# Unsplit float32 operands for 128-column attention products, and a later place for retention's row scaling

## The chip, the core and the metric

The kernel runs on one core of one Trainium2 chip. The metric is the time of one execution on the device in microseconds (us); the kernel before takes 961.94 us, the median of 3 runs (961.93 to 963.8). TensorE (PE in the profile, PEld for its weight loads) multiplies matrices, VectorE (DVE), ScalarE (ACT) and GpSimd (POOL) work on elements, SyncE (SP) issues DMAs; each engine works through its own queue in order.

## The reference

Two layers of a decoder trunk, on 512 tokens of width 1024, all in float32. In each layer one input projection of the normed residual feeds four groups, each 512 wide: retention (4 heads of 128), a Mamba-2 state-space mixer (8 heads of 64), stick-breaking attention (4 heads of 128) and cross-attention to 256 memory tokens (4 heads of 128). Each group is gated, and one output projection maps the concatenation back. The two groups that the change touches:

```
retention, per head, with q, k after rope:
    y[n] = sum over m <= n of  decay(n - m) * (q[n] . k[m]) * v[m]
    y    = (y - mean(y)) / sqrt(var(y) + 1e-6)          # per token, over the head's 128 columns

stick-breaking, per head, with z = q k^T / sqrt(128):
    w[n, m] = exp( z[n, m] - sum over j = m..n-1 of softplus(z[n, j]) )   for m < n, else 0
    y[n]    = sum over m of w[n, m] * v[m]
```

## The kernel before

**Split products.** A float32 matrix `a` is kept as two tiles in the reduced format that TensorE reads (fp32r): `h`, a rounded copy that ScalarE writes, and `l = a - h`, which VectorE writes (`split`, lines 285 to 287). A product is then three matmuls into one bank, h·h, h·l and l·h (`mm3`, lines 280 to 283, all through `mm`, line 278). The input and output projections, which are most of the work, are done so too: `pj<-hTh,wh`, `pj<-hTl,wh` and `pj<-hTh,wl` in the profile, with 512 columns or, for some, 256.

**Causal blocks.** 512 tokens are 4 blocks of 128, so causal products shrink in steps of 128 columns. Stick-breaking computes for query block t the scores against keys 0 to 128(t+1), that is 128, 256, 384 and 512 columns (`sb_head`, lines 629 to 653): three matmuls, then one bf16 matmul that adds the mask to the diagonal block, then Abs, Exp and Ln on ScalarE, a max, a scan and a subtract on VectorE, and a last Exp. `sb_head2` transposes the weights on TensorE (line 661) and splits them, `sb_head3` multiplies them by the values (512 down to 128 columns). Retention (`ret_head`, lines 718 to 733) computes scores of 512 down to 128 columns, splits each, and GpSimd zeroes the upper triangle of the diagonal block in both halves (line 730); `ret_head2` multiplies by the values, and squares and sums. So each head of either kind has one score product and one value product with 128 columns.

**Retention's norm.** `ret_head3` sums the squares over the head's columns with one matmul against a column of ones (`mx<-r,onesr`); its operand is written by VectorE at line 747. The resulting row of 512 goes through `row_rstd` (lines 702 to 716): ScalarE copies it, a DMA folds it to 32 partitions (`t<-r`), GpSimd adds eps and takes the power -0.5 (`t`, lines 710 and 711), a DMA writes it to DRAM (`row<-t`) and a last one broadcasts it to 128 partitions (`r<-row`). Then VectorE multiplies the head's output with it (`scaled`, line 757).

**What sets the order.** The code runs over projections in a fixed order; each projection is one unit, and `defer(n, f)` puts a function off until n units later, so that the attention work lies between projections. That is only a priority: a scheduler in the compiler then chooses, with a model of the engines, the order in which each engine's queue holds the instructions, except where the code asks for program order. Banks of PSUM come from two pools of four, `pj` for projections and `mx` for the rest. Tiles in SBUF come from pools of equal slots: 33 of class `s`, 16 of `y`, 9 of `r`.

Of the kernel before, what the change touches and what calls it, by code (L numbers as in the profile page):

```python
# [11 lines left out]
AF = mybir.ActivationFunctionType  # L12
# [4 lines left out]
P = 128  # L17
SEQ = 512
NT = SEQ // P
# [4 lines left out]
HEADS = 4  # L24
HD = 128
GW = 512
EPS = 1e-6
SCALE = HD ** -0.5
# [100 lines left out]
RP, RJ = 32, 16  # L129
# [34 lines left out]
def v3(ap, a):  # L164
    return ap.rearrange("p (a b) -> p a b", a=a)


class Builder:
# [384 lines left out]
    def scaled_pair(self, b, scale):  # L553
# [58 lines left out]
    def sb_v(self, l):  # L612
        nc = self.nc
        banks = self.proj_a(extra=SSD_H, turns=l == 0)
        if l:
            self.behind(self.turn[3], self.marks[1])
        first = [Pair(self), Pair(self)]
        u = self.tiny(32)
        uv = u.rearrange("p (h c) -> p c h", c=4)
        bias = self.par(l, "dtb", 0, 32).rearrange("p (h c) -> p c h", c=4)  # L620
        for t, b in enumerate(banks):
            p, c = first[t // 2], slice(256 * (t % 2), 256 * (t % 2) + 256)
            self.split(b[:, :256], p.h[:, c], p.l[:, c], p.hf[:, c])
            nc.vector.tensor_add(uv[:, t], b[:, 256:256 + SSD_H], bias[:, t])
        self.defer(1, self.dt_chain, l, u)
        second = [self.pair(b) for b in self.proj_a()]
        return [[first[i], second[i]] for i in range(2)]

    def sb_head(self, h, v):
        nc = self.nc  # L630
        q = self.scaled_pair(self.proj_b(), SCALE)
        k = self.pair(self.proj_b())
        w = [t[:, c] for t, c in self.packed([P * (t + 1) for t in range(NT)], self.buf)]
        for t in range(NT):
            n = P * (t + 1)
            ts = slice(P * t, P * t + P)
            b = self.mx()[:, :n]
            self.mm(b, q.h[:, ts], k.h[:, :n], True, False)
            self.mm(b, q.h[:, ts], k.l[:, :n], False, False)
            self.mm(b, q.l[:, ts], k.h[:, :n], False, False)  # L640
# [12 lines left out]
        return y  # L653

    def sb_head2(self, h, v, w, y):
        nc = self.nc
        wT = self.pairs_packed([SEQ - P * j for j in range(NT)])
# [5 lines left out]
        self.defer(1, self.sb_head3, h, v, wT, y)  # L663

    def sb_head3(self, h, v, wT, y):
        b = self.mx()
        for j in range(NT):
            c = slice(P * j, SEQ)
            self.mm3(b[:, c], *self.vcols(v, j, h), wT[j][0], wT[j][1], j == 0, j == NT - 1)
        self.nc.scalar.copy(y, b)  # L670


    def ret_v(self):

        nc = self.nc
        ginv = self.con("ginv", 16)
        out = [[None, None], [None, None]]
        for half in range(2):
            for i, b in enumerate(self.proj_a()):
                st = self.tiny(4)  # L680
                nc.vector.tensor_reduce(out=st, in_=v3(b, 4), op=ALU.add, axis=AX.X)
                nc.vector.tensor_scalar(out=st, in0=st, scalar1=-1.0 / HD, scalar2=None, op0=ALU.mult)
                vt = self.buf()
                for j in range(4):
                    t, h = 2 * i + j // 2, 2 * half + j % 2
                    nc.vector.tensor_scalar(out=vt[:, P * j:P * j + P], in0=b[:, P * j:P * j + P],
                                            scalar1=st[:, j:j + 1], scalar2=ginv[:, 4 * t + h:4 * t + h + 1],
                                            op0=ALU.add, op1=ALU.mult)
                out[i][half] = self.pair(vt)
        return out  # L690

    def rope(self, b):
        nc = self.nc
        cos, sin = self.con("cos", SEQ), self.con("sin", SEQ)
        A, B = self.buf(), self.buf()
        nc.vector.tensor_tensor(out=B[0:64], in0=b[64:128], in1=sin[64:128], op=ALU.mult)
        nc.vector.tensor_tensor(out=B[64:128], in0=b[0:64], in1=sin[0:64], op=ALU.mult)
        nc.vector.tensor_tensor(out=A, in0=b, in1=cos, op=ALU.mult)
        nc.vector.tensor_add(A, A, B)
        return self.pair(A)  # L700

    def row_rstd(self, row, eps):

# [14 lines left out]
    def ret_head(self, h, v):  # L718
        nc = self.nc
        q = self.rope(self.proj_b())  # L720
        k = self.rope(self.proj_b())
        sc = self.pairs_packed([SEQ - P * c for c in range(NT)])
        for c in range(NT):
            n = SEQ - P * c
            cs, ms = slice(P * c, SEQ), slice(P * c, P * c + P)
            b = self.mx()[:, :n]
            self.mm3(b, k.h[:, ms], k.l[:, ms], q.h[:, cs], q.l[:, cs], True, True)
            self.split(b, *sc[c])
            for d in (sc[c][0][:, :P], sc[c][1][:, :P]):
                nc.gpsimd.affine_select(out=d, in_=d, pattern=[[1, P]], compare_op=ALU.is_ge, fill=0.0, base=0, channel_multiplier=-1)  # L730
        y = self.buf(tag="y")
        self.defer(4, self.ret_head2, h, v, sc, y)
        return y

    def ret_head2(self, h, v, sc, y):
        nc = self.nc
        b = self.mx()
        for c in range(NT):
            self.mm3(b[:, P * c:], *self.vcols(v, c, h), sc[c][0], sc[c][1], c == 0, c == NT - 1)
        nc.scalar.copy(y, b)  # L740
        sq = [self.buf(tag="r")[0:64] for _ in range(2)]
        for i in range(2):
            nc.scalar.activation(sq[i], b[64 * i:64 * i + 64], AF.Square, scale=HD ** -0.5)
        nc.vector.tensor_add(sq[0], sq[0], sq[1])
        z = self.new(512, F32R, "r")
        nc.scalar.copy(z[0:64], sq[0])
        nc.vector.tensor_sub(z[64:128], sq[0], z[0:64].bitcast(F32))
        self.defer(1, self.ret_head3, h, z, y)

    def ret_head3(self, h, z, y):  # L750
        nc = self.nc
        vb = self.mx()[0:1]
        self.mm(vb, self.onesr[:, 0:1], z[:], True, True)
        self.defer(5, self.scaled, y, self.row_rstd(vb, self.con("reps", HEADS * RJ, RP)[:, RJ * h:RJ * h + RJ]))

    def scaled(self, y, rB):
        self.nc.vector.tensor_mul(y, y, rB)


    def dt_chain(self, l, u):  # L760
# [437 lines left out]
```

## Time and profile before

| | |
|---|---|
| median of 3 runs | 961.94 us (961.93 to 963.8) |
| the profiled execution | 961.89 us |
| its span, first to last instruction | 960.2 us |
| lies outside the span | 1.69 us |
| TensorE's mean granted clock | 0.998 |
| stick-breaking, about | 123 to 205 us, and again some 471 us later in layer 2 |
| retention, with the state-space group between, about | 205 to 330 us, and again 471 us later |

A timeline gives start, length, engine, line, operation, tiles written and read, shape, and how many like instructions stand in a row; in brackets the engine's idle time before it and what ended it. TensorE's matmuls are pipelined, and their lengths overlap: how fast it works is read from start to start, not from the lengths. A product of unsplit float32 operands is shown as two matmul records.

### The profile page before, as it was taken

What the parts mean: (1) busy time and instruction counts of PE and PEld (TensorE: products, weight loads), DVE (VectorE), ACT (ScalarE), POOL (GpSimd) and SP (SyncE); (2) the same over time, 40 slices, a digit from 0 to 9 for tenths busy, and PEclk for the clock granted to TensorE, in tenths of its full rate; (3) what the DMA queues carried; (4) which work ended last, traced back from release to release, by engine and by line L of the source; (5) the groups of instructions that cost most, each with busy time, mean ns of one, the idle gap of its engine ahead of it and who ended that gap; (6) DMA issues with size and microseconds to landing.
All of it is one profiled execution on the core that took longest, in us unless ns stands there. A gap on an engine that the chain in (4) does not pass through costs nothing.

```text
span 960.2 us, 13253 instructions
## 1 busy us (share of the span) xinstructions
PE 949.8 (99%) x5151; PEld 812.6 (85%) x5151; DVE 657.4 (68%) x1056; ACT 456.8 (48%) x844; POOL 104.4 (11%) x160
## 2 busy tenths in 40 slices
PE   9999999999999999999999999999999999999997
PEld 7998889988887888888899888898888878888885
DVE  5855567767777796854487465768777968877443
ACT  6544566534554342643465345665344543435341
POOL 1100000001231201100040000000003421102001
PEclk9999999999999999999999999999999999999999
DMA  9442212122232524344344222112222333423502
GB/s 347 149 147 80 88 45 88 45 88 88 91 108 99 165 88 121 115 160 142 120 170 184 89 88 71 62 45 88 77 78 85 134 105 116 120 91 120 195 25 87
DMA packets 26734, 105.79 MB, mean 110 GB/s; under 512 B 4144, under 2 KB 4400, under 8 KB 17456
## 3 DMA queue, kind: packets, MB, share of 16 engines
q10 hardware_dynamic: 10224, 73.44, 21.8%
q1 hardware_dynamic: 16448, 31.52, 10.0%
q8 instruction: 40, 0.66, 0.3%
q14 instruction: 22, 0.18, 0.1%
HBM read 100.63 MB, written 4.28 MB: 109 GB/s over the span
## 4 chain that ended last, share of the span: by engine, by line
PE 88%; DVE 5%; DMA 3%; ACT 1%; issue 1%; POOL 1%; DVEq 0%; SPq 0%; ACTq 0%; POOLq 0%
PE pj L278 65%; PE mx L278 22%; DVE s L647 1%; DMA r<-row 1%; PE mx L599 1%; PE mx L449 1%; DMA mem<-memT 1%; DMA s<-acs 1%; DVE wl L287 1%; DMA t<-r 1%; POOL t L711 1%; DVE s L810 1%; DVE s L646 0%; PE mx L661 0%; DVE s L287 0%
## 5 line engine op out<-in xcount | busy, mean ns | idle before, releaser
L278 PE MATMUL pj<-hTh,wh 128*128 128x512 f32 x704 | 277.5, 394 | 0.0
L278 PE MATMUL pj<-hTl,wh 128*128 128x512 f32 x704 | 276.6, 393 | 0.0
L278 PE MATMUL pj<-hTh,wl 128*128 128x512 f32 x704 | 275.4, 391 | 0.0
L287 DVE TENSOR_TENSOR wl<-raw,wh 128x1024 fp32r<-128x1024 f32 (+2 forms) x155 | 183.7, 1190 | 114.2 <-ACT wh L286 107.3
L286 ACT CAST wh<-raw 128x1024 fp32r<-128x1024 f32 (+2 forms) x155 | 158.0, 1025 | 178.9 <-PE pj L278 153.7
L278 PEld LDWEIGHTS pj<-hTh,wl 128*128 128x128 f32 x704 | 132.3, 188 | 26.7
L278 PEld LDWEIGHTS pj<-hTh,wh 128*128 128x128 f32 x704 | 132.3, 188 | 26.4
L278 PEld LDWEIGHTS pj<-hTl,wh 128*128 128x128 f32 x704 | 132.4, 188 | 25.7
L278 PE MATMUL pj<-wh,s 128*128 128x512 f32 (+1 forms) x384 | 99.8, 355 | 0.0
L278 PE MATMUL mx<-s,s 128*128 128x256 f32 (+4 forms) x616 | 97.5, 310 | 0.3
L278 PEld LDWEIGHTS mx<-s,s 128*128 128x128 f32 (+1 forms) x616 | 84.6, 178 | 12.9 <-issue 3.1
L278 PE MATMUL mx<-wh,s 128*128 128x512 f32 x256 | 79.2, 389 | 0.0
L278 PEld LDWEIGHTS pj<-wh,s 128*128 128x128 f32 x384 | 66.1, 189 | 10.5
L730 POOL TENSOR_SCALAR_AFFINE_SELECT s<-s 128x128 fp32r<-128x128 f32 x64 | 21.2, 363 | 420.6 <-DVE s L287 420.6
L278 PE MATMUL pj<-wl,s 128*128 128x512 f32 (+1 forms) x192 | 63.4, 354 | 0.0
L278 PE MATMUL pj<-wh,hTh 128*128 128x256 f32 (+1 forms) x208 | 60.3, 290 | 0.5 <-DVE s L556 0.5
L287 DVE TENSOR_TENSOR s<-mx,s 128x512 fp32r<-128x512 f32 (+2 forms) x86 | 42.1, 517 | 26.0 <-ACT s L286 25.6
L278 PE MATMUL pj<-wl,hTh 128*128 128x256 f32 (+1 forms) x208 | 59.5, 286 | 0.0
L278 PE MATMUL pj<-wh,hTl 128*128 128x256 f32 (+1 forms) x208 | 58.5, 284 | 0.0
L278 PEld LDWEIGHTS mx<-wh,s 128*128 128x128 f32 x256 | 48.1, 188 | 10.0
L286 ACT CAST s<-mx 128x512 fp32r<-128x512 f32 (+2 forms) x86 | 36.7, 456 | 40.1 <-PE mx L278 24.1
L287 DVE TENSOR_TENSOR s<-y,s 128x512 fp32r<-128x512 f32 x64 | 41.3, 688 | 19.7 <-ACT s L286 14.0
(167 smaller groups left out, 1324.5 us busy)
## 6 DMA issues: line engine op xcount, KB each, us to landing
raw<-wts ACTq DMA_DIRECT2D x69, 1024.0 KB, 4.8
s<-x SPq DMA_DIRECT2D x24, 256.0 KB, 3.7
s<-acs SPq DMA_DIRECT2D x16, 256.0 KB, 6.1
raw<-wts SPq DMA_DIRECT2D x3, 1024.0 KB, 8.3
r<-row SPq DMA_DIRECT2D x12, 256.0 KB, 3.9
s<-acs SPq DMA_DIRECT2D x16, 128.0 KB, 6.7
x<-s SPq DMA_DIRECT2D x8, 256.0 KB, 2.0
out<-s SPq DMA_DIRECT2D x8, 256.0 KB, 2.0
```

Source lines behind the costliest of these rows:

```text
L278: return self.nc.tensor.matmul(out, lhsT, rhs, start=start, stop=stop)
L286: self.nc.scalar.copy(h, src)
L287: self.nc.vector.tensor_sub(l, src, hf)
L449: x = self.nc.tensor.transpose(b[:, P * j:P * j + P], hn[i][:, P * j:P * j + P], self.con("ident", P))
L599: nc.tensor.transpose(b[:, P * t:P * t + P], w[t // 2][:, o:o + P], self.con("ident", P))
L647: nc.vector.tensor_tensor_scan(out=u[:, ::-1], data0=u[:, ::-1], data1=u[:, ::-1], initial=0.0, op0=ALU.add, op1=ALU.bypass)
L711: nc.gpsimd.tensor_tensor(out=c, in0=c, in1=self.mhalf[:RP], op=ALU.pow)
L730: nc.gpsimd.affine_select(out=d, in_=d, pattern=[[1, P]], compare_op=ALU.is_ge, fill=0.0, base=0, channel_multiplier=-1)
L810: nc.vector.scalar_tensor_tensor(out=acc[:, s:], in0=b[:, :SEQ - s], scalar=tap(3 - s), in1=acc[:, s:], op0=ALU.mult, op1=ALU.add)
```

## The change

1. Stick-breaking: the score product of query block 0 is one matmul on unsplit q and k (their first 128 columns, which ScalarE copies from the projection's bank, `first_chunk`); the last value product is one matmul on the unsplit transposed weights (copied by ScalarE, no subtract on VectorE) and an unsplit value tile that ScalarE copies in `sb_v`.
2. Retention: the score product of the last block takes rope's output unsplit; its result is copied by ScalarE alone, with one masking instead of two; the last value product takes it and the unsplit value tile.
3. The stick-breaking weights take slots of class `r` in place of `s`, and `sb_head2` comes 4 units later instead of 3.
4. `scaled` comes 7 units later instead of 5, and its multiply is kept in program order.

```diff
+    def first_chunk(self, b, scale, out):
+        self.nc.scalar.activation(out, b[:, :P], AF.Copy, scale=scale)
+        return out
 def sb_v(self, l):
-        second = [self.pair(b) for b in self.proj_a()]
-        return [[first[i], second[i]] for i in range(2)]
+        f = self.buf()
+        nc.scalar.copy(f[:, :256], banks[3][:, :256])
+        banks = self.proj_a()
+        second = [self.pair(b) for b in banks]
+        nc.scalar.copy(f[:, 256:], banks[1][:, 256:])
+        return [first[0], second[0]], [first[1], second[1]], f
 def sb_head(self, h, v):
-        q = self.scaled_pair(self.proj_b(), SCALE)
-        k = self.pair(self.proj_b())
-        w = [t[:, c] for t, c in self.packed([P * (t + 1) for t in range(NT)], self.buf)]
+        f = self.buf(3 * P)
+        b = self.proj_b()
+        q = self.scaled_pair(b, SCALE)
+        q.f = self.first_chunk(b, SCALE, f[:, :P])
+        b = self.proj_b()
+        k = self.pair(b)
+        k.f = self.first_chunk(b, 1.0, f[:, P:2 * P])
+        w = [t[:, c] for t, c in self.packed([P * (t + 1) for t in range(NT)], lambda: self.buf(tag="r"))]
...
+            if t == 0:
+                self.mm(b, q.f, k.f, True, False)
+            else:
...
-        self.defer(3, self.sb_head2, h, v, w, y)
+        self.defer(4, self.sb_head2, h, v, w, f[:, 2 * P:], y)
 def sb_head2(self, h, v, w, f, y):
-            self.split(b[:, P * j:], *wT[j])
+            if j == NT - 1:
+                nc.scalar.copy(f, b[:, P * j:])
+            else:
+                self.split(b[:, P * j:], *wT[j])
 def sb_head3(self, h, v, wT, f, y):
+            if j == NT - 1:
+                self.mm(b[:, c], v[2][:, HD * h:HD * h + HD], f, False, True)
 def ret_head(self, h, v):
+            if c == NT - 1:
+                self.mm(b, k.f[:, ms], q.f[:, cs], True, True)
+                sc.append(k.f[:, :P])
+                nc.scalar.copy(sc[c], b)
...
-            for d in (sc[c][0][:, :P], sc[c][1][:, :P]):
+            for d in (sc[c],) if c == NT - 1 else (sc[c][0][:, :P], sc[c][1][:, :P]):
 def ret_head2(self, h, v, sc, y):
+            if c == NT - 1:
+                self.mm(b[:, P * c:], v[2][h // 2][:, HD * (h % 2):HD * (h % 2) + HD], sc[c], False, True)
 def ret_head3(self, h, z, y):
-        self.defer(5, self.scaled, y, self.row_rstd(...))
+        self.defer(7, self.scaled, y, self.row_rstd(...))
 def scaled(self, y, rB):
-        self.nc.vector.tensor_mul(y, y, rB)
+        self.tc.keep_in_program_order(self.nc.vector.tensor_mul(y, y, rB))
```

The edits also shift every line number: line 757 becomes 792, 744 becomes 778, 747 becomes 781, 810 and 813 become 845 and 848, 643 becomes 660.

VectorE's queue in retention of layer 1, before, where the norm of the fourth head is prepared. `y_2632` is the third head's output, `r_2915` its broadcast row, `r_3008` and `r_3013` are the fourth head's squares (lines 744 and 747).

```order
L287 TENSOR_TENSOR wl_3147<-raw_2946,wh_3146 128x1024
L757 TENSOR_TENSOR y_2632<-y_2632,r_2915 128x512
L744 TENSOR_TENSOR r_3008<-r_3008,r_3009 64x512
L813 SCALAR_TENSOR_TENSOR s_3114<-s_3114,s_3113 128x512
L810 SCALAR_TENSOR_TENSOR s_3152<-pj_3121,hp_776,s_3152 128x511
L747 TENSOR_TENSOR r_3013<-r_3008,r_3013 64x512
```

The same place of the queue now; `r_2978` and `r_2983` are the fourth head's squares, `y_2433` is the second head's output and `r_2679` its row.

```order
L778 TENSOR_TENSOR r_2978<-r_2978,r_2979 64x512
L845 SCALAR_TENSOR_TENSOR s_3083<-pj_3054,hp_778,s_3083 128x509
L287 TENSOR_TENSOR wl_3118<-raw_2918,wh_3117 128x1024
L781 TENSOR_TENSOR r_2983<-r_2978,r_2983 64x512
L848 SCALAR_TENSOR_TENSOR s_3084<-s_3084,s_3083 128x512
L792 TENSOR_TENSOR y_2433<-y_2433,r_2679 128x512
```

The multiply ahead of the fourth head's two steps is gone; the one behind them is of the second head, not the third. The third head's (`y_2613`) stands ten places further on.

ScalarE's queue ahead of the first stick-breaking scores, before; `mx_1317` is the bank of the 128-column scores, `pj_1281` that of k.

```order
L286 CAST s_1268<-mx_1263 128x512
L286 CAST s_1277<-mx_1272 128x512
L286 CAST s_1310<-pj_1281 128x512
L286 CAST wh_1555<-raw_1249 128x1024
L643 ACTIVATE s_1314<-mx_1317 128x128
```

The same place now; `mx_1323` is the bank of the 128-column scores, `pj_1286` that of head 0's k, `pj_1379`, `pj_1423` and `pj_1508` those of q and k of head 1 and q of head 2.

```order
L286 CAST s_1315<-pj_1286 128x512
L555 ACTIVATE s_1410<-pj_1379 128x512
L561 ACTIVATE s_1197<-pj_1286 128x128
L561 ACTIVATE s_1370<-pj_1379 128x128
L286 CAST s_1452<-pj_1423 128x512
L286 CAST wh_1533<-raw_1253 128x1024
L555 ACTIVATE s_1539<-pj_1508 128x512
L660 ACTIVATE r_1320<-mx_1323 128x128
```

Ahead of the first Abs now stand the two copies of line 561 and the casts of three later projections.

## Rows read from the trace of the kernel before

**Rows 1.** The page: busy time by engine, and the granted clock in 40 slices.

```profile
PE 949.8 (99%) x5151; PEld 812.6 (85%) x5151; DVE 657.4 (68%) x1056; ACT 456.8 (48%) x844; POOL 104.4 (11%) x160
...
PEclk9999999999999999999999999999999999999999
```

**Rows 2.** Waits of PE: who waits for whom, us in total, times, longest.

```profile
PE mx L278 <- DVE r L747: 1.8, 2, 0.9
...
PE pj L278 <- DVE s L556: 0.5, 2, 0.2
```

**Rows 3.** Groups by shape, PE: the attention products with 128 columns.

```profile
L278 PE MATMUL mx<-s,s 128*128 128x128 f32 x176 | 27.9, 268 | 0.1
```

**Rows 4.** Timeline, PE: a retention score product with 128 columns, then projections.

```profile
275.34 0.44 PE L278 MATMUL mx<-s,s 128*128 128x128 f32 x3
275.62 0.44 PE L278 MATMUL pj<-hTh,wh 128*128 128x512 f32 x1
275.90 0.40 PE L278 MATMUL pj<-hTl,wh 128*128 128x512 f32 x1
276.14 0.39 PE L278 MATMUL pj<-hTh,wl 128*128 128x512 f32 x1
```

**Rows 5.** Timeline, PE: one split 128-column matmul alone between projections with 256 columns.

```profile
153.18 0.22 PE L278 MATMUL mx<-s,s 128*128 128x128 f32 x1
153.24 0.34 PE L278 MATMUL pj<-wh,hTh 128*128 128x256 f32 x1
153.42 0.28 PE L278 MATMUL pj<-wl,hTh 128*128 128x256 f32 x1
```

**Rows 6.** Timeline, PE: unsplit products of the state-space group, transposes, then projections.

```profile
361.50 1.05 PE L278 MATMUL mx<-s,s 128*128 128x128 f32 x8
362.38 0.49 PE L891 MATMUL mx<-consts,s 128*128 128x128 f32 x3
362.63 0.49 PE L278 MATMUL pj<-hTh,wh 128*128 128x512 f32 x1
...
363.19 0.39 PE L278 MATMUL pj<-hTh,wl 128*128 128x512 f32 x1
```

**Rows 7.** Waits of DVE: the multiply at line 757.

```profile
DVE y L757 <- DMA r<-row: 20.2, 6, 5.4
```

**Rows 8.** Timeline, DVE, around that multiply in layer 1.

```profile
298.72 1.23 DVE L287 TENSOR_TENSOR wl<-raw,wh 128x1024 fp32r<-128x1024 f32 x1
305.37 0.69 DVE L757 TENSOR_TENSOR y<-y,r 128x512 f32<-128x512 f32 x1 [5.42 <-DMA r<-row]
...
307.95 0.69 DVE L747 TENSOR_TENSOR r<-r,r 64x512 fp32r<-64x512 f32 x1
```

**Rows 9.** Timeline, PE, in the same stretch.

```profile
307.41 0.39 PE L278 MATMUL pj<-hTl,wh 128*128 128x512 f32 x1
308.69 0.39 PE L278 MATMUL mx<-r,onesr 128*1 128x512 f32 x1 [0.89 <-DVE r L747]
...
311.68 0.39 PE L278 MATMUL pj<-hTh,wl 128*128 128x512 f32 x1
312.07 1.13 PE L278 MATMUL mx<-s,s 128*128 128x128 f32 x8
```

**Rows 10.** Chain of waits, window 280 to 310 us: start, length, what.

```profile
300.94 4.41 DMA r<-row
```

**Rows 11.** Timeline, PE, in the middle of stick-breaking.

```profile
150.57 0.38 PE L278 MATMUL pj<-wh,hTh 128*128 128x256 f32 x1 [0.24 <-DVE s L556]
150.79 0.28 PE L278 MATMUL pj<-wl,hTh 128*128 128x256 f32 x1
```

**Rows 12.** Groups by shape, ACT, 123 to 205 us: Abs on 128 columns.

```profile
L643 ACT ACTIVATE s<-mx 128x128 f32<-128x128 f32 x4 | 1.1, 278 | 4.3 <-PE mx L278 4.1
```

**Rows 13.** Groups by shape, DVE, 123 to 330 us: the subtract of a split.

```profile
L287 DVE TENSOR_TENSOR s<-pj,s 128x512 fp32r<-128x512 f32 x3 | 2.0, 682 | 0.0
```

**Rows 14.** Busy time in a window of stick-breaking: us, then PE, PEld, DVE, ACT.

```profile
126.00:167.00 41.00, 40.65 (x248) 35.31 (x247) 30.35 (x53) 29.05 (x65) 0.00 (x0) 1.00 0.22 78
```

More of the change, by code (lines that the diff above doesn't have):

```diff
@@ L637, in sb_head @@
             b = self.mx()[:, :n]
-            self.mm(b, q.h[:, ts], k.h[:, :n], True, False)
-            self.mm(b, q.h[:, ts], k.l[:, :n], False, False)
-            self.mm(b, q.l[:, ts], k.h[:, :n], False, False)
+            if t == 0:
+                self.mm(b, q.f, k.f, True, False)
+            else:
+                self.mm(b, q.h[:, ts], k.h[:, :n], True, False)
+                self.mm(b, q.h[:, ts], k.l[:, :n], False, False)
+                self.mm(b, q.l[:, ts], k.h[:, :n], False, False)
             self.mm(b[:, P * t:n], self.b16[:, 0:P], self.b16[:, P:2 * P], False, True)
@@ L651, in sb_head, with sb_head2 @@
         y = self.buf(tag="y")
-        self.defer(3, self.sb_head2, h, v, w, y)
+        self.defer(4, self.sb_head2, h, v, w, f[:, 2 * P:], y)
         return y
-    def sb_head2(self, h, v, w, y):
+    def sb_head2(self, h, v, w, f, y):
         nc = self.nc
-        wT = self.pairs_packed([SEQ - P * j for j in range(NT)])
+        wT = self.pairs_packed([SEQ - P * j for j in range(NT - 1)])
         for j in range(NT):
@@ L661, in sb_head2, with sb_head3 @@
                 nc.tensor.transpose(b[:, P * t:P * t + P], w[t][:, P * j:P * j + P], self.con("ident", P))
[L662 to L665 removed]
+            if j == NT - 1:
+                nc.scalar.copy(f, b[:, P * j:])
+            else:
+                self.split(b[:, P * j:], *wT[j])
+        self.defer(1, self.sb_head3, h, v, wT, f, y)
+    def sb_head3(self, h, v, wT, f, y):
         b = self.mx()
@@ L668, in sb_head3 @@
             c = slice(P * j, SEQ)
-            self.mm3(b[:, c], *self.vcols(v, j, h), wT[j][0], wT[j][1], j == 0, j == NT - 1)
+            if j == NT - 1:
+                self.mm(b[:, c], v[2][:, HD * h:HD * h + HD], f, False, True)
+            else:
+                self.mm3(b[:, c], *self.vcols(v, j, h), wT[j][0], wT[j][1], j == 0, False)
         self.nc.scalar.copy(y, b)
@@ L676, in ret_v @@
         ginv = self.con("ginv", 16)
-        out = [[None, None], [None, None]]
+        out = [[None, None], [None, None], []]
         for half in range(2):
@@ L689, in ret_v @@
                 out[i][half] = self.pair(vt)
+            out[2].append(vt[:, 2 * P:])
         return out
@@ L699, in rope @@
         nc.vector.tensor_add(A, A, B)
-        return self.pair(A)
+        p = self.pair(A)
+        p.f = A
+        return p
     def row_rstd(self, row, eps):
@@ L721, in ret_head @@
         k = self.rope(self.proj_b())
-        sc = self.pairs_packed([SEQ - P * c for c in range(NT)])
+        sc = self.pairs_packed([SEQ - P * c for c in range(NT - 1)])
         for c in range(NT):
@@ L726, in ret_head @@
             b = self.mx()[:, :n]
-            self.mm3(b, k.h[:, ms], k.l[:, ms], q.h[:, cs], q.l[:, cs], True, True)
-            self.split(b, *sc[c])
-            for d in (sc[c][0][:, :P], sc[c][1][:, :P]):
+            if c == NT - 1:
+                self.mm(b, k.f[:, ms], q.f[:, cs], True, True)
+                sc.append(k.f[:, :P])
+                nc.scalar.copy(sc[c], b)
+            else:
+                self.mm3(b, k.h[:, ms], k.l[:, ms], q.h[:, cs], q.l[:, cs], True, True)
+                self.split(b, *sc[c])
+            for d in (sc[c],) if c == NT - 1 else (sc[c][0][:, :P], sc[c][1][:, :P]):
                 nc.gpsimd.affine_select(out=d, in_=d, pattern=[[1, P]], compare_op=ALU.is_ge, fill=0.0, base=0, channel_multiplier=-1)
@@ L738, in ret_head2 @@
         for c in range(NT):
-            self.mm3(b[:, P * c:], *self.vcols(v, c, h), sc[c][0], sc[c][1], c == 0, c == NT - 1)
+            if c == NT - 1:
+                self.mm(b[:, P * c:], v[2][h // 2][:, HD * (h % 2):HD * (h % 2) + HD], sc[c], False, True)
+            else:
+                self.mm3(b[:, P * c:], *self.vcols(v, c, h), sc[c][0], sc[c][1], c == 0, False)
         nc.scalar.copy(y, b)
@@ L753, in ret_head3 @@
         self.mm(vb, self.onesr[:, 0:1], z[:], True, True)
-        self.defer(5, self.scaled, y, self.row_rstd(vb, self.con("reps", HEADS * RJ, RP)[:, RJ * h:RJ * h + RJ]))
+        self.defer(7, self.scaled, y, self.row_rstd(vb, self.con("reps", HEADS * RJ, RP)[:, RJ * h:RJ * h + RJ]))
     def scaled(self, y, rB):
-        self.nc.vector.tensor_mul(y, y, rB)
+        self.tc.keep_in_program_order(self.nc.vector.tensor_mul(y, y, rB))
     def dt_chain(self, l, u):
```

## The prediction

> **What bounds the kernel now.** I read the page first: TensorE is busy 949.8 of 960.2 us, and every slice shows a granted clock of 9 tenths or more, the 2.4 GHz level [rows 1]. So only two things shorten the kernel: less work on TensorE, or fewer of the moments in which it stands. The waits of PE come second, and the two that this change touches are short: 1.8 us at the matmul with the column of ones, until VectorE's line 747, and 0.5 us at projections, until line 556 [rows 2]. Third, since lengths of pipelined matmuls overlap (27.9 us is the sum for the 176 records of the 128-column products, and not what they cost [rows 3]), I took the price of a product from the timeline, from start to start.
>
> **Products: removed and added.** 4 heads of each kind and 2 layers make 16 heads, each with one score and one value product of 128 columns: 32 products, 96 split matmuls that go, out of the 176 records of [rows 3]; the other 80 belong to other stages. In their place stand 32 unsplit products, two records each.
>
> What three split ones cost: the block starts at 275.34, and the third projection after it at 276.14 [rows 4], that is 0.80 us with two projections in it. A product with 512 columns takes 0.23 us from start to start (the one with the ones and the 12 projections after it, from 308.69 to 311.68, make 13 steps in 2.99 us [rows 9]). 0.80 - 2 x 0.23 = 0.34 us for three, or 0.11 each. That the block seems to pass in 0.28 us hides a part: the next projection takes 0.28 too.
>
> A single one shows the same: it starts at 153.18, the next projection only 0.06 later, but that one lasts 0.18 where 0.12 is usual [rows 5], so 0.12 in all. The column stream alone would be the 0.06; the weights of a new operand, loaded for each matmul, make it twice as much.
>
> "TensorE: Matmul & The Clock Gate" of the Trainium skill (Back-to-back issue gap) gives N / 2.4 + 2.5 ns for a matmul that stands by itself, 56 ns for 128 columns; its section LDWEIGHTS (loading the stationary operand) gives P / 1.2, 107 ns for 128 columns of weights. By the gap alone three split matmuls would cost 0.17 us and be cheaper than two unsplit records, which speaks against this change; the row sides with the weight load.
>
> What an unsplit one costs: eight records of unsplit products start at 361.50 and the transposes after them at 362.38, 0.11 each; over all 11 records up to 363.19 it is 1.69 - 2 x 0.23 = 1.23 us, 0.112 each [rows 6]. Two make 0.224 us. The gain per product is 0.34 - 0.224 = 0.116 us. Nothing in the trace shows a block of only two between split matmuls; the refill of about 0.10 at the end of [rows 6] (0.32 for the first projection) is in the 1.23 already, spread over 11. Charged whole to two records, 0.22 + 0.10 = 0.32, the gain is 0.02; if the second record passes in 0.06, as a single one does before its successor starts [rows 5], and nothing is refilled, a pair takes 0.17 and the gain is 0.17. Bounds for 32 products: 0.6 to 5.4 us. I take 32 x 0.116 = 3.7 us, since the transposes in [rows 6] stand in the same position and the average over the block holds.
>
> **The multiply at line 757.** It waits 20.2 us in 6 of its 8 places for the broadcast row [rows 7]. Mostly that costs nothing; in retention of each layer it does. In layer 1 VectorE stands 5.42 us until 305.37, because the transfer `r<-row` takes from 300.94 to 305.35 [rows 8, 10]. Behind it in the queue stand line 744 and, at 307.95, line 747 of the fourth head. TensorE reaches the matmul with the ones too early and starts it at 308.69 in place of 307.41 + 0.23 = 307.64: 1.05 us lost [rows 9], the 0.89 shown as idle and a refill. Layer 2 gives the second of the two waits of [rows 2], so 2.1 us. The convolution that was held up too comes 0.16 us late at 312.07 (311.68 + 0.23 = 311.91) [rows 9], some 0.3 us in both layers.
>
> In the new queue no multiply stands ahead of lines 778 and 781 of the fourth head; the one behind them is the second head's, whose row was asked for one head earlier. The third head's comes ten places later, some 6 us by the durations around 0.6 us in [rows 8], hence at about 308 to 311 us or after, when its row has landed at 305.35. So the wait doesn't move elsewhere, and I count 2.1 + 0.3 = 2.4 us. The bounds: nothing, if ScalarE's squares or another transfer are as late as VectorE was (1.28 us lie between 307.41 and 308.69, and nothing before shows a spare arrival), and 2.8 us, if both refills vanish. What is late next is TensorE itself. The scaled output is used only by the output projection's side, after retention; that it comes 18 us later for a head hides behind the state-space work.
>
> **Stick-breaking: two ways to be late.** What goes: a stop of 0.24 us at 150.57 and a refill (0.22 instead of 0.12 to the next start) [rows 11]; with layer 2 some 0.7 us, 0.5 of it in [rows 2]. VectorE loses 16 subtracts on 128 columns (0.29 us or less each, after the 0.68 that 512 columns take [rows 13]), GpSimd 8 maskings; neither bounds. What comes: 20 copies on ScalarE, 16 of them of 128 columns at about 0.28 us [rows 12], in a stretch where it is busy 29.05 of 41 us [rows 14]. Two of these now stand ahead of a head's first score product, each behind the subtract of the same bank. For head 0 the chain after the last transposes before it is two casts, a subtract of 0.68 and a copy of 0.28, some 2.2 us, and TensorE has 24 projections of 0.23, 5.5 us, in the meantime: hidden. For heads 2 and 3 I followed the new queues by hand with durations from the trace, and found 1.5 to 2.5 us left; the narrowest place is the last, where the transposes of head 3 and the value products of head 2 alternate, with 0.2 us left. If that cover is gone, each head costs what it lacks. I take -0.6 us for the whole, between -1.3 (all small stops go) and +2 (four of the eight heads late by half a us).
>
> **Sum.** 961.89 - 3.7 - 2.4 - 0.6 = 955.2 us for the profiled execution, 0.05 below the median of the runs, which is nothing here.
>
> **Rivals.**
> *Stop stays.* The matmul with the ones waits for something else at the same time, ScalarE's squares or the queue that the scheduler filled anew. For it: only the last releaser is seen. Against it: 5.42 us of VectorE's queue are freed, five times the stop. 961.9 - 3.7 - 0.6 = 957.6.
>
> *The switch eats the gain.* Each unsplit pair pays its own refill, 0.02 us gained per product: 961.9 - 0.6 - 2.4 - 0.6 = 958.3. For it: 0.32 us to the first projection in [rows 6]. Against: it follows transposes there.
>
> *Streams, not loads.* If the weights of the split matmuls were loaded under other work, each would cost 0.06 as its start suggests [rows 5]; three are 0.18, two unsplit records 0.22, and 32 x 0.04 = 1.3 us are lost: 961.9 + 1.3 - 2.4 - 0.6 = 960.2. The isolated gap in "TensorE: Matmul & The Clock Gate" of the Trainium skill (Back-to-back issue gap), taken as the rule, would have it so. Against it stands the 0.18 us of the next projection in the same rows.
>
> *ScalarE becomes the wait in stick-breaking (slower).* The copy of q and k stands in ScalarE's queue between casts and Abs, and the first scores of a head wait for it; from 6.7 / 8 = 0.84 us per head on the whole gain is spent. With the subtract of 0.68, the copies of 0.28 twice and a Cast in the way a late head could cost 1.2 to 1.5 us: 8 x 1.3 = 10.4, 961.9 - 6.1 + 10.4 = 966.2. For it: ScalarE has only 12 us in 41 free [rows 14], and the casts of three more projections now stand ahead of the first Abs. Against: 5.5 us of projections ahead of each head's scores.
>
> **How the numbers follow.** Forecast 0.70, with 953.4 to 957.2 as its own range; stop stays 0.09; the switch eats the gain 0.08; streams 0.05; ScalarE 0.06; the rest, 0.02, is left to what I don't see. The range reaches from 953.3, where the products gain 4.9, the stops 2.6 and stick-breaking 1.1, to 959.4, which takes in the two rivals around 958 with 1.2 us on their far side. A measurement of this kernel tells 0.2%, 1.9 us, from no change. Faster by more than that, under 960.0: forecast, stop, switch and a third of streams, less a little, 0.86; same: two thirds of streams and parts of ScalarE, 0.08; slower 0.06.
>
> **What would show it.** In the new profile: 80 + 64 = 144 records in the group of [rows 3]; in the timeline of a retention score product two records and 0.224 us in place of 0.34; no wait of PE for line 781; multiplies at line 792 with little or no wait; no new stop of PE in the stretch of stick-breaking above 0.3 us. I am wrong if PE waits there for line 561 or 680 of ScalarE, or if the first projection after an unsplit pair takes 0.32 us.

## The result and the profile after

The changed kernel takes 955.97 us, the median of 6 runs (953.88 to 956.29), against 961.93 us (961.43 to 963.8) for the kernel before in as many: a ratio of 0.9932, 95% interval 0.9919 to 0.9944. Forecast were 955.2 us, with 953.3 to 959.4. The median lies 0.8 us above the forecast, and the profiled execution, for which it was made, 1.1 us; but the terms that the forecast summed are not those that gave it.

The profiled execution took 956.29 us, 5.60 less than before's. First the page of the changed kernel, the busy times and the granted clock by slice, which answer to [rows 1].

```profile
PE 945.6 (99%) x5119; PEld 810.8 (85%) x5119; DVE 655.7 (69%) x1040; ACT 459.7 (48%) x864; POOL 100.7 (11%) x152
...
PEclk9999999999999999999999999999999999999999
```

TensorE has 32 records fewer (96 gone, 64 come) and is still busy all the time. Its waits, to be held against [rows 2]: both are gone, and what is left belongs to the first 9 us.

```profile
PE pj L278 <- ACT s L492: 1.4, 1, 1.4
PE mx L278 <- POOL b L190: 1.2, 1, 1.2
```

The price of a product. This is the timeline of TensorE in the changed kernel from the unsplit score product of a retention head on; the first row holds a split matmul with 384 columns, three with 256 and the unsplit pair.

```profile
275.20 0.93 PE L278 MATMUL mx<-s,s 128*128 128x384 f32 x6
275.89 0.48 PE L278 MATMUL pj<-hTl,wh 128*128 128x512 f32 x1
276.20 0.40 PE L278 MATMUL pj<-hTh,wl 128*128 128x512 f32 x1
276.44 0.40 PE L278 MATMUL pj<-hTh,wh 128*128 128x512 f32 x1
276.67 0.40 PE L278 MATMUL pj<-hTl,wh 128*128 128x512 f32 x1
...
278.97 0.39 PE L278 MATMUL pj<-hTh,wl 128*128 128x512 f32 x1
```

The pair starts at 275.75, inside the first row. The first projection follows 0.14 us later, but lasts 0.31 to the next start, and the 12 projections after it do not run at 0.227 at once: from 275.89 to 278.97 there are 13 in 3.08 us, 13 x 0.227 = 2.95 would be the undisturbed ones. The same place before, from the block of three at 278.62 on:

```profile
278.90 0.44 PE L278 MATMUL pj<-hTh,wh 128*128 128x512 f32 x1
...
281.92 0.39 PE L278 MATMUL pj<-hTl,wh 128*128 128x512 f32 x1
```

0.28 us for the block and 3.02 for 13 projections. So three split matmuls cost 0.28 + 3.02 - 2.95 = 0.35 us, and the unsplit pair 0.14 + 3.08 - 2.95 = 0.27. A product gains 0.08 us, not 0.116.

The weight loads of the block of [rows 4], before, show what bounds split matmuls of 128 columns. From the block's second load, at 275.35, to that of the second projection, at 275.68, there are three steps in 0.33 us, without idle time between the loads; from there on the steps are the projections' own 0.23 us.

```profile
275.12 0.53 PEld L278 LDWEIGHTS mx<-s,s 128*128 128x128 f32 x3
275.56 0.19 PEld L278 LDWEIGHTS pj<-hTh,wh 128*128 128x128 f32 x1
275.68 0.19 PEld L278 LDWEIGHTS pj<-hTl,wh 128*128 128x128 f32 x1
275.91 0.19 PEld L278 LDWEIGHTS pj<-hTh,wl 128*128 128x128 f32 x1
```

The multiply, in the timeline of VectorE, layer 1; it answers to [rows 8]:

```profile
296.67 0.67 DVE L778 TENSOR_TENSOR r<-r,r 64x512 f32<-64x512 f32 x1
...
299.47 0.69 DVE L781 TENSOR_TENSOR r<-r,r 64x512 fp32r<-64x512 f32 x1
300.18 0.69 DVE L848 SCALAR_TENSOR_TENSOR s<-s,s 128x512 f32<-128x512 f32 x1
300.79 0.68 DVE L792 TENSOR_TENSOR y<-y,r 128x512 f32<-128x512 f32 x1
```

Nothing waits: the fourth head's squares stand ahead of the multiply, and its row has landed. TensorE's matmul with the ones, against [rows 9], starts without idle time:

```profile
304.18 0.39 PE L278 MATMUL pj<-hTl,wh 128*128 128x512 f32 x1
304.40 0.40 PE L278 MATMUL mx<-r,onesr 128*1 128x512 f32 x1
```

Stick-breaking, the window of [rows 14]: TensorE is busy 41.00 of 41 us, where it was 40.65.

```profile
126.00:167.00 41.00, 41.00 (x253) 35.85 (x253) 30.89 (x51) 28.66 (x69) 0.00 (x0) 1.00 0.19 65
```

And one thing that the forecast did not have, the start. Both kernels begin with 37 small matmuls that keep TensorE busy until the first weights are there. Windows of 2 us of the changed kernel (columns as in [rows 14], then the granted clock as a share of 2.4 GHz, DMA share, GB/s):

```profile
10.00:12.00 2.00, 1.94 (x8) 1.15 (x8) 1.87 (x5) 2.00 (x5) 0.00 (x0) 0.95 0.98 406
12.00:14.00 2.00, 2.00 (x11) 2.00 (x11) 1.23 (x1) 1.35 (x3) 0.00 (x0) 0.50 1.04 399
14.00:16.00 2.00, 2.00 (x14) 2.00 (x13) 1.98 (x2) 2.00 (x5) 0.35 (x1) 0.70 1.05 406
```

and of the kernel before:

```profile
12.00:14.00 2.00, 2.00 (x19) 2.00 (x18) 1.41 (x2) 1.35 (x3) 0.00 (x0) 1.00 1.05 402
```

The changed kernel's clock stands at 1.2 GHz for some 3 us, and 11 products pass in 2 us where 19 did. Nothing in the change touches this place.

To keep the start apart, the experiments are compared by a **body time**: from the start of the 101st projection matmul to that of the last one, of 3504 in every kernel (22.45 to 909.98 us before, 887.53 us; 24.16 to 904.38 after, 880.21 us). By it the change is worth 7.32 us, and 1.71 us of that were lost at the start of the profiled execution: 7.32 - 1.71 = 5.61.

### The profile page after: what moved, and what is told of

Its sections match the earlier page's. It is cut to its first block, busy times and chain, and to the rows that moved or that the text cites. A ratio compares the mean times of both kernels' runs of the same rounds, so it can differ in the third digit from the quotient of the medians.

```text
span 954.5 us, 13196 instructions
## 1 busy us (share of the span) xinstructions
PE 945.6 (99%) x5119; PEld 810.8 (85%) x5119; DVE 655.7 (69%) x1040; ACT 459.7 (48%) x864; POOL 100.7 (11%) x152
## 4 chain that ended last, share of the span: by engine, by line
PE 98%; DMA 1%; DVEq 0%; ACT 0%; SPq 0%; issue 0%; POOLq 0%; POOL 0%; ACTq 0%; DVE 0%
PE pj L278 73%; PE mx L278 23%; PE mx L678 1%; PE mx L604 1%; PE mx L449 1%; DMA mem<-memT 1%; PE mx L906 0%; PE mx L926 0%; DVEq L1229 0%; ACT s L1075 0%; POOLq L1229 0%; ACT s L492 0%; SPq L340 0%; SPq L1111 0%; POOL t L419 0%
## 5 line engine op out<-in xcount | busy, mean ns | idle before, releaser
L278 PE MATMUL mx<-s,s 128*128 128x128 f32 (+4 forms) x568 | 90.5, 316 | 0.0
L278 PEld LDWEIGHTS mx<-s,s 128*128 128x128 f32 (+1 forms) x568 | 76.9, 177 | 10.3 <-issue 2.8
L761 POOL TENSOR_SCALAR_AFFINE_SELECT s<-s 128x128 fp32r<-128x128 f32 (+1 forms) x56 | 18.7, 360 | 419.2 <-ACT s L756 387.0
L287 DVE TENSOR_TENSOR s<-mx,s 128x512 fp32r<-128x512 f32 (+2 forms) x70 | 38.0, 569 | 22.1 <-ACT s L286 21.8
L286 ACT CAST s<-y 128x512 fp32r<-128x512 f32 x64 | 36.6, 617 | 30.4 <-PE mx L278 22.0
```

The source lines that it names most:

```text
L278: return self.nc.tensor.matmul(out, lhsT, rhs, start=start, stop=stop)
L286: self.nc.scalar.copy(h, src)
L287: self.nc.vector.tensor_sub(l, src, hf)
```

## The experiments

The ratios are to runs of the kernel before on the same chip, each with its 95% interval. "Body" is the change of the body time in the one profiled execution against that of the kernel before. The runs of the kernel before that stood beside the experiments had medians between 962.4 and 963.4 us, so small differences are read from the body.

**The later multiply alone.**

```diff
-        self.defer(5, self.scaled, y, self.row_rstd(...))
+        self.defer(7, self.scaled, y, self.row_rstd(...))
-        self.nc.vector.tensor_mul(y, y, rB)
+        self.tc.keep_in_program_order(self.nc.vector.tensor_mul(y, y, rB))
```

> The kernel before with the fourth part of the change alone: scaled put off by 7 units and its multiply in program order. In VectorE's queue no multiply by a row that is still in flight stands ahead of the fourth head's squares. Theory of the sum: the stop at the matmul with the ones goes in both layers, 2 x 1.05 us and some 0.3 us behind it, so 961.9 - 2.4 = 959.5 us (959.2 to 959.9), and PE has no wait for line 747. Rival (the stop stays, since something else is as late): 961.9 us, with a wait of PE for another engine at about 308.7 us. Rival (the stop goes only because the products take less of VectorE): 961.9 us with the same wait.

Measured: 958.57 us (958.32 to 958.95), ratio 0.9951 (0.9931 to 0.9972), body -2.83 us. PE has no wait for line 747; the two for line 556 stay at 0.5 us. The first theory holds: by itself this edit takes out the stop, and gives 0.4 us more than the forecast's 2.4. By the starts of the same projections in both kernels, 1.3 us of it lie at each of the two stops and 0.2 at a third place, in layer 2: the state-space group's transposes (line 871) start 0.38 us after the projection ahead of them before, at 811.86 us, and 0.23 here.

**The change without the later multiply.** The same lines the other way round, on the changed kernel.

> The changed kernel without the fourth part: scaled put off by 5 units, not in program order. The multiply by the third head's row stands again right ahead of the fourth head's squares. By the price that the changed kernel's timeline shows for an unsplit pair (about 0.265 us where three split ones take 0.346, 32 x 0.08 = 2.6 us) and with the small stops in stick-breaking gone (1.8 us), 4.4 us less than before after the start-up: 957.5 us with before's start-up, 959.2 with the slower start-up that the changed kernel's profile shows. By the prediction's price (0.116 per product) and -0.6 in stick-breaking: 957.6. The two differ in the parts: in retention, 16 products give 1.3 us against 1.9. PE waits for line 781 twice, some 0.9 us each.

Measured: 954.16 us (953.86 to 955.39), ratio 0.9905 (0.9884 to 0.9926), body -7.36 us. The expectation of two stops was wrong, and so were both theories: without its fourth part the change is worth as much, -7.36 against -7.32. VectorE's queue shows why (timeline of this kernel):

```profile
295.51 0.67 DVE L778 TENSOR_TENSOR r<-r,r 64x512 f32<-64x512 f32 x1
299.77 0.69 DVE L792 TENSOR_TENSOR y<-y,r 128x512 f32<-128x512 f32 x1 [3.59 <-DMA r<-row]
...
302.89 0.68 DVE L781 TENSOR_TENSOR r<-r,r 64x512 fp32r<-64x512 f32 x1
```

The multiply still waits 3.59 us, but its row lands at 299.77, and line 781 is through at 303.6, before TensorE wants it:

```profile
286.75 0.40 PE L278 MATMUL mx<-r,onesr 128*1 128x512 f32 x1
304.68 0.40 PE L278 MATMUL mx<-r,onesr 128*1 128x512 f32 x1
```

The row belongs to the third head, whose matmul with the ones starts it. Here that matmul is at 286.75, 263.4 us after the body's start; before it was at 290.53, 268.1 us after it. It is 4.7 us earlier, but the fourth head's has moved with it, so the place alone does not settle it. What counts is the distance: the fourth follows 17.9 us behind the third, where before it would have followed after 17.3 without its stop, and the row lands 13.0 us behind the third, where it took 14.8. The section on the prediction compares all kernels by this.

**Retention's products alone.** The hunks of `ret_v`, `rope`, `ret_head` and `ret_head2`, on the kernel before.

> The kernel before with the second part alone: retention's 16 products of 128 columns take unsplit operands; stick-breaking and scaled as before. From the last projection of stick-breaking to the end of the state-space work, both layers: 16 x 0.08 = 1.3 us less if a pair costs 0.265 us, 1.9 us if 0.224 (the prediction), 0.3 us if the refill is paid whole (0.32), a loss of 0.6 if a split one costs 0.06. The stop at the matmul with the ones stays (0.9 us each). The stretch of stick-breaking stays as before, with its stop of 0.24 us at 150.6.

Measured: 962.13 us (961.03 to 965.36), ratio 0.9993 (0.9975 to 1.0011), body -0.30 us. The stops grew:

```profile
PE mx L278 <- DVE r L758: 2.5, 2, 1.5
...
PE pj L278 <- DVE s L556: 0.5, 2, 0.2
PE mx L882 <- DVE s L824: 0.2, 1, 0.2
```

2.5 us against 1.8 and a new 0.2, some 1.1 us with their refills by estimate; 0.30 + 1.1 = 1.4 us for 16 products, 0.087 each (0.077 if the idle time alone is counted). So a pair costs about 0.27, not 0.224, not 0.32, and most of the gain of the products was given back at the row's transfer: TensorE comes to the fourth head's matmul no later than before, and the row lands 14.9 and 15.3 us behind the third head's, where it took 14.8.

**The third part alone: slots of class r, transposes after 4 units instead of 3.**

```diff
-  w = [... self.packed([P * (t + 1) for t in range(NT)], self.buf)]
+  w = [... self.packed([P * (t + 1) for t in range(NT)], lambda: self.buf(tag="r"))]
-        self.defer(3, self.sb_head2, h, v, w, y)
+        self.defer(4, self.sb_head2, h, v, w, y)
```

> The kernel before with the third part alone: the stick-breaking weights in slots of class r, and their transposes 4 units later instead of 3; all products split. If the order that this makes is what takes the stops out of stick-breaking, its stretch is 0.8 to 0.9 us shorter per layer and PE waits there for nobody: 960.2 us. If the products' shorter work on VectorE and ScalarE does it, the stops stay: 961.9 us.

Measured: 957.39 us (957.03 to 959.51), ratio 0.9940 (0.9924 to 0.9956), body -4.38 us, with all products split. More than either theory: the stops of stick-breaking are gone, and those at the matmul with the ones as well. The third head's matmul with the ones stands 263.2 us after the body's start, much as in the kernel without the later multiply, and the fourth head's 18.7 us behind it.

**The two halves of the third part.** First the later transposes alone, then the slots alone.

> The kernel before with the stick-breaking transposes 4 units later instead of 3, all else as before (weights in class s, products split). Third part as a whole gave 4.4 us after the start-up. If the later transposes are what gives it, 4.4 us here (4.0 to 4.6), and no wait of PE for line 556 or for line 747; if the slots of class r give it, nothing.

Measured: 961.17 us (960.54 to 962.89), ratio 0.9980 (0.9967 to 0.9994), body +0.16 us. It trades stops: these are the waits of PE beside those of the start.

```profile
PE mx L661 <- DVE s L287: 1.2, 2, 0.6
...
PE mx L278 <- DVE r L747: 0.6, 1, 0.6
PE pj L278 <- DVE s L686: 0.5, 2, 0.2
```

> The kernel before with the stick-breaking weights in slots of class r and the transposes 3 units later as before. If the slots give the 4.4 us of the third part, they are here and PE waits neither for line 556 nor for 747; if the later transposes give it, nothing, and the stops of 0.24 us and 0.9 us are there as before. If both are needed, something between.

Measured: 956.90 us (956.74 to 958.14), ratio 0.9937 (0.9917 to 0.9958), body -4.67 us, and no wait of PE after the start. With split products the slots do all of it. The third head's matmul with the ones is at 286.48, again 263.1 us after the body's start, and the fourth head's 18.7 us behind it.

**The change without its third part.** Slots `s`, 3 units, everything else as changed.

> The changed kernel without its third part: stick-breaking weights in class s again, transposes after 3 units; the unsplit products and the later scaled stay. Counted from a projection after the start-up to the end. If the third part alone takes the stops out of stick-breaking, they stay here (PE waits for line 556 or a split in its stretch), and the gain is 2.6 for the products and 2.8 for scaled, 5.4 us. If the products take them out, 7.2 us, as the changed kernel has. If the third part is worth its 4.4 us beside scaled as well, only 2.9 us are left.

Measured: 958.69 us (957.84 to 959.0), ratio 0.9957 (0.9941 to 0.9973), body -4.03 us. A new wait appears, of PE for the copies that the change adds:

```profile
PE pj L278 <- ACT s L561: 1.7, 2, 0.9
...
PE mx L278 <- DVE s L287: 0.7, 2, 0.3
```

In ScalarE's queue a copy of line 561 stands behind the eviction of a head's result, which waits for the value product (timeline of ScalarE, this kernel):

```profile
168.47 0.58 ACT L693 COPY y<-mx 128x512 f32<-128x512 f32 x1 [0.70 <-PE mx L278]
168.95 0.28 ACT L561 ACTIVATE s<-pj 128x128 f32<-128x128 f32 x1
```

and the bank that it reads is the one that the next projection is waiting for. 2.6 + 2.8 = 5.4 would be the parts; 1.4 us are missing, since these stops cost more than the small ones of before, in whose place they stand. It is the rival on ScalarE, at another spot: not the first scores of a head but a projection waits.

**An unsplit pair behind a pair.** Each `self.mm` of unsplit operands is written twice.

> The changed kernel with each of the 32 unsplit products issued twice into the same bank (so those scores and values count double). A second pair directly behind the first costs two records of 0.112 us if TensorE's time per record is all there is: 32 x 0.224 = 7.2 us more after the start-up, and the refill of the next projection is paid once. If each pair carries a refill of its own, 32 x 0.265 = 8.5 us. If the column stream bounds it (0.06 each), 3.8 us.

Measured: 960.94 us (960.52 to 961.85), ratio 0.9985 (0.9974 to 0.9995), body -0.46 us, that is +6.86 against the changed kernel, 0.214 for each further pair. That is what two records cost where they stand behind others; the first pair's 0.27 holds the refill.

**One split matmul for three.** On the kernel before, h by h alone at the 32 places.

> The kernel before with one matmul, h by h, in place of the three at each of the 32 products of 128 columns (the products with l are left out). If each split matmul costs its weight load, 0.115 us, 64 fewer make 7.3 us less after the start-up, as far as no new stop appears; if each costs its column stream, 0.06 us, 3.8 us less. Stops in stick-breaking (0.24 us twice and its neighbours) and at the matmul with the ones (0.9 us twice) as before.

Measured: 954.01 us (952.28 to 957.3), ratio 0.9914 (0.9888 to 0.9941), body -5.40 us. Here too the stop ate a part: PE waits 3.8 us for the fourth head's squares instead of 1.8, and behind the longer stop the clock falls. The third head's matmul with the ones stands 264.5 us after the body's start, 3.6 earlier than before, and yet the stops are longer: the fourth head's would follow after 16.6 us, and the row lands after 15.4, in layer 2 after 17.2. The timeline of TensorE in layer 2 of this kernel, then its windows:

```profile
773.96 0.39 PE L278 MATMUL mx<-r,onesr 128*1 128x512 f32 x1 [2.77 <-DVE r L757]
...
774.89 0.63 PE L278 MATMUL pj<-hTh,wl 128*128 128x512 f32 x1
775.32 0.63 PE L278 MATMUL pj<-hTh,wh 128*128 128x512 f32 x1
```

```profile
770.00:774.00 4.00, 1.23 (x7) 0.69 (x6) 2.10 (x4) 0.00 (x0) 0.00 (x0) 1.00 0.21 52
774.00:776.00 2.00, 2.00 (x7) 1.63 (x8) 1.97 (x3) 0.44 (x1) 0.00 (x0) 0.72 0.00 0
776.00:778.00 2.00, 2.00 (x6) 1.52 (x6) 1.97 (x4) 2.00 (x5) 0.00 (x0) 0.50 0.00 0
```

The price is read from its timeline, as above: at 276.12 the single matmul, the first projection at 276.18, and after 0.28 us the next.

```profile
276.18 0.45 PE L278 MATMUL pj<-hTh,wl 128*128 128x512 f32 x1
276.46 0.39 PE L278 MATMUL pj<-hTh,wh 128*128 128x512 f32 x1
```

0.06 + 0.05 of refill and some 0.03 in the projections behind, 0.14 us. A split matmul of 128 columns does not pass in 0.06; that rival is out.

**The start: 49 small matmuls instead of 37,** on the changed kernel and on the one before.

> The changed kernel with 49 matmuls of warm-up instead of 37. In the profile of the changed kernel TensorE's warm-up ends at 7.25 us, it idles 1.36 us, and its clock is granted at 0.50 from 12 to 14 us; before it ends at 8.24 us, idles 0.15 us, and the clock stays at 1.00. If the idle time is what costs the 1.5 us in the first 50 projections, they are gone: 954 us in all rounds, with a spread below 1 us. If the clock falls at random or by the slow first projections (8 matmuls with 0.4 us from start to start), the runs scatter between 954 and 957 as before. Where the warm-up is now too long it puts off the first projection by up to 1.3 us.

Measured: 954.08 us (953.94 to 954.44), ratio 0.9912 (0.9895 to 0.9929), body -7.32 us as in the changed kernel. No version that computes every product had a lower median, and all its runs lie within 0.5 us. Its windows:

```profile
10.00:12.00 2.00, 1.97 (x12) 1.57 (x13) 1.55 (x4) 1.60 (x3) 0.00 (x0) 1.00 0.97 400
12.00:14.00 2.00, 2.00 (x19) 2.00 (x18) 1.20 (x2) 1.42 (x2) 0.00 (x0) 1.00 1.05 403
```

The clock stays at 2.4 GHz. With the idle time ahead of the first projections filled, the 101st projection matmul starts at 21.97 us instead of 24.16: the 1.71 us are back, and 0.5 more.

The idle time alone does not decide. The kernel with the slots alone, above, has 37 small matmuls, stood 1.02 us at this place and kept its clock:

```profile
9.32 3.19 PE L278 MATMUL pj<-s,wh 128*128 128x256 f32 x8 [1.02 <-ACT s L492]
```

```profile
12.00:14.00 2.00, 1.99 (x16) 1.88 (x16) 1.55 (x3) 1.34 (x3) 0.00 (x0) 1.00 1.05 403
```

The kernel without the later multiply stood only 0.60 and 0.22 us and lost it: 0.80, 0.50 and 0.85 in the three windows from 10 to 16 us. In the five profiles with such a fall the 37 small matmuls had got the full clock by 5.1 us after the span's start; in the six others with 37, at 5.5 us or later. So an execution can lose the clock there whatever the change, and why an early rise goes with the fall is not shown.

> The kernel before with 49 matmuls of warm-up instead of 37. With the idle time ahead of the first projections filled, the start-up no longer decides: all rounds within 0.6 us, at 961.3 (the lowest of the kernel before) to 961.9 us, and the difference from the changed kernel with the same warm-up (954.08) is the 7.3 us that the timelines give after the start-up. If the longer warm-up helps only the changed kernel, runs of 963 us and more stay.

Measured: 963.29 us (961.6 to 968.78), ratio 1.0011 (0.9994 to 1.0029), body +0.55 us. For the kernel before the longer warm-up does nothing: its runs scatter as they did, so the start alone does not make their scatter. Its stops at the matmul with the ones were 1.9 us in this profile.

**Only what had been worth something.** Unsplit products, slots of class r, 49 small matmuls; transposes after 3 units, multiply after 5.

> Only what the runs so far found to be worth something: the unsplit products of both kinds and the stick-breaking weights in slots of class r, with 49 matmuls of warm-up; transposes after 3 units and scaled after 5, not kept in order, as in the kernel before. If the later transposes and the later scaled add nothing, 7.3 us less than before after the start-up, as the changed kernel has, and 953.9 to 954.5 us. If they are needed beside the products, a stop of PE of 0.3 us or more shows in stick-breaking or at the matmul with the ones, and the time is 955 us or more.

Measured: 964.18 us (961.78 to 966.15), ratio 1.0012 (0.9997 to 1.0026), body +0.44 us. The reading that parts of this change add up was wrong. Both kinds of stop are there at once:

```profile
PE mx L278 <- DVE r L781: 3.4, 2, 2.3
PE pj L278 <- ACT s L561: 1.7, 2, 0.9
...
PE mx L278 <- DVE s L287: 0.7, 2, 0.3
```

The third head's matmul with the ones is late again, 267.7 us after the body's start, the fourth head's would follow after 17.2 us, and the row lands 14.9 us behind the third's (16.2 in layer 2):

```profile
304.49 0.69 DVE L792 TENSOR_TENSOR y<-y,r 128x512 f32<-128x512 f32 x1 [5.56 <-DMA r<-row]
```

Against the change without its fourth part this kernel differs in the unit of the transposes (and in the warm-up, which leaves the body alone); so beside unsplit products those later transposes are worth 7.36 + 0.44 = 7.8 us, and beside split ones nothing (-4.38 us with them, -4.67 without).

## Why the prediction was right, and where not

**What bounds the kernel.** Right: TensorE without stops, after as before.

**Products: forecast -3.7 us, measured -2.6.** The direction and the mechanism hold: split matmuls are bound by their weight loads (0.35 us for three, 0.14 for one, each with its refill), unsplit ones pass at 0.11 a record (0.214 for a pair behind a pair). The section LDWEIGHTS (loading the stationary operand) of "TensorE: Matmul & The Clock Gate" in the Trainium skill gives P / 1.2, by estimate 107 ns for 128 columns of weights, and 0.35 us for three, with loads 0.11 us apart, agree with it; the 56 ns, its gap for a matmul that stands by itself, are met only between the first two starts of a block (0.06 us at 275.34 before), and the next steps are 0.11 us. The term was mis-sized in one step, "the average over the block holds": the 11 records of [rows 6] share one refill, a pair bears it alone. That refill is 0.31 instead of 0.23 for the first projection, as the second rival had it, and the prediction had named 0.32 there as a sign that it is wrong; but the second record passes in 0.03 on the way, and then the next ten projections lose some 5 ns each. At 0.27 instead of 0.224 a product gains 0.08, and 32 x 0.08 = 2.6 us. That is one place taken for all 32; at the other places of the changed kernel where 13 projections with 512 columns follow, a pair costs 0.25 to 0.27.

**The stop at the multiply: forecast -2.4, and gone.** The size was nearly right (2.6 us at the two stops, by the run with this edit alone). The reason was not the whole one: the forecast gave the gain to the new place of the multiply, and the run without that edit lost nothing. The stop can be taken out by a later multiply or by a row that lands sooner ahead of the fourth head's matmul; the change does both, and they count once. In the kernels with the multiply after 5 units two distances tell whether TensorE stops (us, layer 1 and layer 2, read from the timelines; the first is the start of the third head's matmul with the ones to that of the fourth's, less the stop):

| kernel | third to fourth matmul | third matmul to its row's landing | stop |
|---|---|---|---|
| before | 17.3, 17.3 | 14.8, 14.8 | 0.9, 0.9 |
| retention's products alone | 17.2, 17.2 | 14.9, 15.3 | 1.0, 1.5 |
| one split matmul for three | 16.6, 16.6 | 15.4, 17.2 | 1.0, 2.8 |
| the last run | 17.2, 17.2 | 14.9, 16.2 | 1.0, 2.3 |
| later transposes alone | 18.7, 18.9 | 14.0, 16.3 | none, 0.6 |
| third part alone | 18.7, 18.7 | 14.1, 15.3 | none |
| slots alone | 18.7, 18.7 | 13.8, 13.7 | none |
| the change without the later multiply | 17.9, 17.9 | 13.0, 11.6 | none |

From the landing to the end of the fourth head's squares VectorE took another 2.1 to 3.8 us; where that end comes after the distance of the first column, TensorE stops. That the new order changes both distances the prediction left out: it compared the queues only around the multiply.

**Stick-breaking: forecast -0.6, measured about -1.8.** By start-to-start distances the stops of before in this stretch were 0.5 us at 150.57 [rows 11] and 0.4 at 166.23, with their equals in layer 2, and all are gone. The second, in TensorE's timeline before:

```profile
165.84 0.27 PE L661 MATMUL mx<-consts,s 128*128 128x128 f32 x1
166.23 0.73 PE L278 MATMUL mx<-s,s 128*128 128x512 f32 x2
```

The forecast counted the first in part and not the second. Why they are gone was left open, and it is the third part, which the forecast priced at nothing: beside split products the slots alone do it, and beside unsplit ones the later transposes are needed as well, since the last run, with the slots and without these, stops.

**The rival on ScalarE,** with 0.06, did not happen in the changed kernel, but it is real: with the transposes a unit earlier, in the new slots or the old ones, PE waits 0.85 us in each layer for the new copies. The cover that I found by following the queues is the order that the later transposes make.

**Sum.** -2.6 (products) - 2.6 (the stops at the ones) - 0.2 (the transposes at 811.86 us of before, on time in the changed kernel too) - 1.8 = -7.2 of the -7.32 in the body; 0.1 is not assigned. -7.32 and +1.71 from the start, in the profiled execution, give -5.6. That the forecast of -6.7 came out near was in part luck: a term too large, terms too small and a loss at the start that it did not have nearly cancelled.

**What stays open.** Why slots of another class let the scheduler set retention's matmuls with the ones further apart was not tried; the runs show only that they do. The fast end of the changed kernel's own runs (953.88) lies where all runs of the longer warm-up lie, which fits the clock at the start, but only one of its executions was seen in full.

## What to carry to other kernels

Price a short block by all that follows it until the rhythm is back, and at its own length: an average over a longer block hides the refill. Where a scheduler orders the queues, parts of a change do not add up; compare, in the new queues, the distance from every producer of the critical chain to the instruction that waits for it, and not only the instruction that was moved. When work is taken from the engine that bounds, look at each transfer that it will now reach too early.

## What the runs showed of the hardware

Half clock followed two kinds of gap. At the start, TensorE stood 1.36 us and then got eight products 0.4 us apart; from 12 us on the granted clock was 0.50, for some 3 us. In the middle of a kernel a stop of 2.77 us, in the run with one split matmul, was followed by 0.72 and 0.50 in the next two windows, and eight projections took 0.43 us instead of 0.23: a stop of 2.8 us cost 8 x 0.2 = 1.6 us more. The stops of 0.9 us before cost no clock, nor did one of 2.34 us in layer 2 of the last run. The first kind is not sure to cost it: a gap of 1.02 us at the start, followed by products at the same pace, did not.

Kernels that stop for the broadcast row scatter most: 961.6 to 968.8 (before with the longer warm-up), 961.8 to 966.2 (the last run), 961.0 to 965.4 (retention's products alone). Of those that don't, some are steady, 958.3 to 959.0 (the later multiply alone), 960.5 to 961.9 (each pair twice) and 953.9 to 954.4 (the longer warm-up), and some that lost the clock at the start in their profile lie between, 953.9 to 956.3 (the changed kernel) and 957.0 to 959.5 (the third part alone). The row's broadcast of 256 KB, twelve times in each of the 14 profiles, took between 3.0 and 6.2 us. A transfer that varies so would make the first group scatter; that it does is not shown, since one execution of each kernel was seen in full.
